# A decoder layer's FFN head reordered: the shift written to the result at the end, pair 3's first weights loaded two tiles later, pair 2's X and Y worked on behind h's last row tile

## The chip, the cores and the metric

The kernel runs on one core of a Trainium2 chip. The metric is the device time of one execution in microseconds (us). The core has these engines: TensorE (PE in the profile; PEld is its weight load), VectorE (DVE), ScalarE (ACT), GpSimd (POOL) and SyncE (SP). SP, ACT and POOL also issue DMA transfers; each of them has a queue of its own that is worked off in order, and all queues share 16 DMA engines. A name with a q behind it (SPq, POOLq) is an engine's instruction queue.

## What is computed

One layer of a decoder on an input of 512 tokens by 1024 channels, float32:

```
proj = x @ w_in                       # q, k, v, pool_in, gate logits
y_attn = moba_attention(q, k, v) @ w_branch_attn
y_pool = multiscale_pool(pool_in) @ w_branch_pool
mixed = sigmoid(g0) * y_attn + sigmoid(g1) * y_pool
h = layer_norm(ALPHA * x + mixed @ w_out, ln1_g, ln1_b)
a, u = split(h @ w_ffn_in)            # 2 x 2816 columns
a = causal_dwconv(a, conv_w, conv_b)  # width 3
f = (gelu(a) * u) @ w_ffn_out
out = layer_norm(ALPHA * h + f, ln2_g, ln2_b)
```

The last line adds the row `ln2_b` to every row of the result. In this text that row, repeated over all tokens, is called the shift.

## The kernel before

**Precision.** Every float32 operand is split into a high part (`hi`, rounded by ScalarE at L76) and a low part (`lo`, the difference, taken by VectorE at L77). A product is then three matmuls, high by high, high by low and low by high (`mm3`, L246; L248, L251 and L252 in the profile).

**Weights.** All weights of the layer are cut into tiles of 128 x 1024 (512 KB) and numbered in the order of use in the list `chunks`. `fetch` (L135) takes the next one: it issues the load into a raw tile on SP (L151), and splits it into a slot of a ring of five pairs (`RING`). Raw tiles have the tag `wraw`, with three slots; raw tiles of the plain weights (`wraw` in the profile) and of the A weights of pairs (`araw`) share them. `weights(i)` fetches up to three tiles ahead of tile i (`LEAD`), but not past `state["limit"]`.

**Pairs.** Most weight tiles come in pairs whose two products are made with seven half-size products in place of eight (a Strassen scheme, `seven`, L293). A pair (key `("f", n)` in the FFN) needs four tiles from its two raw halves: A, X, D and Y. A is a plain load into an `araw` tile (`fetch_raw`, L188). X is a difference, made by two loads into one tile: a plain one on SP (L196), and an adding one on POOL (L198). D is half a tile, loaded on SP (L190). Y needs no load; it is made from X and A by two VectorE additions (L212). A's raw tile is kept until Y has been made in it. `load_ahead(i)` (L158) issues the raw loads of pairs ahead of tile i: A up to 4 tiles, X up to 5, D up to 6 (`AHEAD`), except for keys with a number of their own in `EARLY`. For A the number counts only where the pair before also is a pair, else it is 0. The other operand's forms, called T1 to T4, are made on VectorE and split (`t_form`, L266).

**The FFN's head.** After the attention and the merge, the product with `w_out` is made in four row tiles of 128 tokens (`wo_mm`). Row tile i is normalised on VectorE (`ln1_vec`, L833), then transposed on TensorE into `hT`, split, and copied to `hraw` (`ln1_T`, L843). During the last row tile's product the first five FFN tiles are fetched: pair 2's A, and then four plain tiles (0 to 3, columns a and u of FFN blocks 0 and 1). Four plain tiles are multiplied in two halves of the tokens: first with t1 (row tiles 0 and 1; L934 to L938), later with t2 (row tiles 2 and 3; L954 to L957). Between the halves stand pair 2's A (`seven_open`) and row tile 3's transposition (L940). `h_forms(r)` makes the four forms of one half of h's rows: `h_forms(0)` uses row tiles 0 and 2, `h_forms(1)` row tiles 1 and 3. Then all pairs from 2 to 18 follow (L965).

**What sets the order.** The program is handed to a scheduler which orders each engine's instructions by their place in the program and by when its own model of time has them ready. Two means write an order by hand: `tc.issue_after(ins)`, in which every instruction made on `ins`'s engine stands behind `ins` in that engine's queue, and `tc.keep_in_program_order`. Loads can be placed far ahead of their place in the program; that holds for the write of the shift at L931, which has nothing to wait for.

**The FFN's end.** `w_ffn_out` is multiplied in seven products (`product`, L1038), with weights partly loaded on SP (L231, `wraw<-in_w_fo`) and partly made in the tile `tw` by adding loads on POOL (L236). `ln_rows(2)` (L758) loads the scale and shift rows of the second norm, repeated over 128 partitions, into the tile `lnb` on POOL, and POOL scales the first of them (L761). The result's row tiles 0 and 1 are finished early: `scale_out` (L807) scales the centred rows on ScalarE and adds them to the result in memory with an adding DMA on POOL (L812), which is why the shift must stand in the result's first 256 rows before. Row tiles 2 and 3 add the shift on the core (L820, L829, L803) and are stored by SP and ACT (L1065).

Of the kernel before, what the change touches and what calls it, by code (L numbers as in the profile page):

```python
# [14 lines left out]
P = 128  # L15
S = 512
D = 1024
# [14 lines left out]
LEAD = 3  # L32
RING = 5
# [10 lines left out]
HALVED = 2 * SEVEN[0]  # L44
TAILED = 2
AHEAD = {"A": 4, "X": 5, "D": 6}
EARLY = {("i", 1, "X"): 3, ("i", 1, "D"): 2, ("i", 2, "A"): 3, ("i", 2, "X"): 2, ("i", 2, "D"): 3}
SUMMED = (("i", 1),)
PRODUCTS = ("T3", "B11", "B21", "T1", "T2", "B22", "T4")

# [2 lines left out]
def layer_kernel(ctx: ExitStack, tc: tile.TileContext, xT, x, w_v, w_c, rel_bias, invcnt, w_group,  # L53
                 pscale, w_br, w_out, lnr, w_fi, convp, w_fo, out):
    nc = tc.nc
# [9 lines left out]
    def bank(name):  # L65
        return ps.tile([P, S], F32, tag="ps", name=name)
# [5 lines left out]
    def split(hi, lo, src, copy=None):  # L72
        if copy:
            copy(hi, src)
        else:
            state["hi"] = nc.scalar.activation(hi, src, AF.Copy)  # L76
        state["lo"] = nc.vector.tensor_tensor(lo, src, hi.bitcast(F32), op=ALU.subtract)  # L77
        return state["lo"]
# [5 lines left out]
    at = {}  # L84
    pair_of = {}
# [25 lines left out]
    FI0 = len(chunks)  # L111
# [16 lines left out]
    def slot(i, n, near=False):  # L128
        o = BESIDE if near else 0
        return tuple(wp.tile([P, SLOT], F32R, tag=f"w{q}", name=f"w{q}{i}", bufs=RING)[:, o:o + n]  # L130
                     for q in ("hi", "lo"))

    state = {"next": 0, "limit": WO0 - 1}

    def fetch(pool=None, early=None):  # L135
        i = state["next"]
        state["next"] = i + 1
        load_ahead(i)
        if isinstance(chunks[i], tuple):
            ready[i] = (fetch_fo if i >= FO0 else fetch_seven)(i, *chunks[i])  # L140
            return
        raw = wp.tile([P, D], F32, tag="wraw", name=f"wraw{i}", bufs=3)
        if pool is None:
            hi, lo = slot(i, D, FI0 < i <= FI0 + HALVED)
        else:
            hi = pool.tile([P, D], F32R, name=f"whi{i}")
            lo = pool.tile([P, D], F32R, name=f"wlo{i}")
        parts = 2 if early else 1
        for c in range(parts):
            sl = slice(c * (D // parts), (c + 1) * (D // parts))  # L150
            (nc.scalar if early else nc.sync).dma_start(raw[:, sl], chunks[i][:, sl])  # L151
            split(hi[:, sl], lo[:, sl], raw[:, sl])
            if c == 0 and early:
                state["w0"] = raw[:, sl]
                early()
        ready[i] = (hi, lo)

    def load_ahead(i):  # L158
        for q, ahead in AHEAD.items():
            while coming[q]:  # L160
                key = coming[q][0]
                n, f = key
                lead_ = EARLY.get((n, f, q), ahead)
                if not homes.get((n, q)) or at[n, f, q] > i + (lead_ if q != "A" or (n, f - 1) in pair_of else 0):
                    break
                with ExitStack() as held:
                    if (n, f, q) == ("i", 1, "X"):
                        held.enter_context(tc.issue_after(state["neg"].ins))
                    if (n, f, q) in (("i", 1, "D"), ("i", 2, "A"), ("i", 2, "X"), ("i", 2, "D")):
                        held.enter_context(tc.issue_after(state["plain"].ins))  # L170
                    if (n, f, q) == ("i", 2, "X"):
                        held.enter_context(tc.issue_after(state["sum"].ins))
                    fetch_raw(coming[q].pop(0), q)
# [8 lines left out]
    homes = {(n, "A"): araw for n in "igf"}  # L182

    def fetch_raw(key, q):
        a, u = pair_of[key]
        r = raws[key, q] = homes[key[0], q](key[1])
        if q == "A":
            nc.sync.dma_start(r, a)  # L188
        elif q == "D":
            nc.sync.dma_start(r, u[:, S:])  # L190
        elif key in SUMMED:
            state["plain"] = nc.sync.dma_start(r[:, :S], u[:, :S])
        else:
            v = r.rearrange("p (a c) -> p a c", a=2)
            (pst, pn), (est, _) = u.ap
            state["plain"] = nc.sync.dma_start(  # L196
                v, bass.AP(tensor=u.tensor, offset=u.offset, ap=[[pst, pn], [0, 2], [est, S]]))
            state["acc"] = nc.gpsimd.dma_start(  # L198
                v, bass.AP(tensor=a.tensor, offset=a.offset, ap=[[pst, pn], [u.offset + S - a.offset, 2], [est, S]]),
                accum_op=ALU.add)  # L200
# [40 lines left out]
    def weights(i):  # L241
        while state["next"] <= min(i + LEAD, state["limit"]):
            fetch()
        return ready[i]
# [41 lines left out]
    def seven_open(key, whole, y):  # L286
        ba, bc = (bank(f"s{q}{key[0]}{key[1]}") for q in "ac")
        s_mm(key, "A", 0, block(whole, k1, t1), ba[:, 256:], True)
        nc.scalar.activation(y, ba[:, 256:], AF.Copy)
        s_mm(key, "A", 1, block(whole, k2, t1), bc[:, :256], True)  # L290
        return ba, bc
# [314 lines left out]
    ap = attn.enter_context(tc.tile_pool(name="ap", bufs=2, reuse_waits="tile"))  # L606
# [109 lines left out]
    def gate_done(f, ba, u):  # L716
        if f < KT - 1:
            for br, v, scale in ((0, ba, 1.0), (1, u, -1.0)):
                nc.scalar.activation(v, v, AF.Sigmoid, scale=scale)
                nc.vector.tensor_tensor(branch[f, br], branch[f, br], v, op=ALU.mult)  # L720
            merged(f, branch[f, 0], branch[f, 1])
        else:
            for br, v, scale in ((0, ba, 1.0), (1, u, -1.0)):
                gslot[8 * br + f] = unused.pop(0)
                nc.scalar.activation(gslot[8 * br + f], v, AF.Sigmoid, scale=scale)
# [6 lines left out]
    for f in range(GSEVEN, KT):  # L732
        if f == KT - 1:
# [3 lines left out]
              lambda ba, u, f=f: gate_done(f, ba, u), first_half if f == KT - 1 else None)  # L737
# [20 lines left out]
    def ln_rows(r):  # L758
        t = hw.tile([P, 2, D], F32, tag="lnb", name=f"lnb{r}")
        nc.gpsimd.dma_start(t, bass.AP(tensor=lnr.tensor, offset=lnr.offset + r * D, ap=[[0, P], [D, 2], [1, D]]))  # L760
        nc.gpsimd.tensor_scalar(t[:, 0, :], t[:, 0, :], -0.5, None, op0=ALU.mult)  # L761
        return t

    lnb = ln_rows(0)
# [78 lines left out]
    def ln1_T(i):  # L843
        for n in range(2):
            b = bank(f"ht{i}_{n}")
            for k in range(4):
                kt = 4 * n + k
                nc.tensor.transpose(b[:, k * P:(k + 1) * P], xs[:, i, kt * P:(kt + 1) * P], ident)
            b = b.rearrange("p (a c) -> p a c", a=4)
            split(hT_hi[:, 4 * n:4 * n + 4, i * P:(i + 1) * P], hT_lo[:, 4 * n:4 * n + 4, i * P:(i + 1) * P], b)  # L850
            nc.scalar.activation(hraw[:, 4 * n:4 * n + 4, i * P:(i + 1) * P], b, AF.Copy)
# [30 lines left out]
    def fi_mm(j, b, t):  # L882
        wh, wl = split3(weights(at["f", j // 2, "au"[j % 2]]), KT)
        for kt in range(KT):
            mm3(b[:, t], (wh[:, kt, :], wl[:, kt, :]), (hT_hi[:, kt, t], hT_lo[:, kt, t]), kt == 0, kt == KT - 1)
# [41 lines left out]
    coming["X"], late_x = [k for k in coming["X"] if k[1] in firsts], [k for k in coming["X"] if k[1] not in firsts]  # L927
    coming["D"], late_d = [k for k in coming["D"] if k[1] in firsts], [k for k in coming["D"] if k[1] not in firsts]
    load_ahead(FI0 + HALVED)
    shift = bass.AP(tensor=lnr.tensor, offset=lnr.offset + 3 * D, ap=[[0, 2 * P], [1, D]])  # L930
    nc.gpsimd.dma_start(out[:2 * P, :], shift)  # L931
    hb = {}
    head_f = SEVEN[0]
    for j in range(HALVED):  # L934
# [3 lines left out]
            ln1_T(2)  # L938
    opened = seven_open(("f", head_f), (hT_hi, hT_lo), homes["f", "P"](head_f))
    ln1_T(3)  # L940

    rows = [slice(r * P, r * P + P) for r in range(2)]

    def h_forms(r):
        blocks_ = [hraw[:, k, t.start + rows[r].start:t.start + rows[r].stop] for k in (k1, k2) for t in (t1, t2)]
        for n in parts:
            t_form(n, {n: tuple(v[:, :, rows[r]] for v in tt[n])}, *blocks_)

    with tc.issue_after(state["norm"].ins):
        h_forms(0)  # L950
        state["limit"] = FI0 + RING
        fetch()
    h_forms(1)
    for j in range(HALVED):  # L954
        state["limit"] = FI0 + RING + 1 + j
        weights(state["limit"] - LEAD)
        fi_mm(j, hb[j], t2)  # L957
        if j % 2:
            gated(j // 2, hb[j - 1], hb[j])
# [98 lines left out]
    def gather_all(bs, *parts):  # L1058
        for i in range(2):
            for row, col, sign, first, last in parts:  # L1060
                gather(2 * row + i, col * S, (col + 1) * S, bs[i], sign, first, last)
# [19 lines left out]
    gather(3, S, D, bank_a[1], 1, False, False)  # L1081
    product(5, bank_d, False)
    lnb = ln_rows(2)
    gather_all(bank_d, (0, 0, -1, False, True))
    for i in range(2):
        scale_out(i)
# [86 lines left out]
```

## Time and profile before

| | |
|---|---|
| time, median of 3 executions (lowest, highest) | 636.46 us (634.88, 636.7) |
| the profiled execution's own time | 635.43 us |
| its span, from the first instruction to the last | 633.6 us |
| instructions | 10413 |
| mean granted clock of TensorE in it | 0.992 |
| moved by DMA | 107.70 MB, mean 170 GB/s |

Times in the profile count from the start of the span. A row of the timeline holds the start, the duration, the engine, the line of the code, the operation, the tile written, the tiles read, the number of instructions of one kind that are merged in it, and in brackets the engine's idle time ahead of it and what ended that. A row of the list of waits holds the engine and the line that waited, what it waited for, the sum of the waits, their number, and the longest. A row of the windows holds the stretch and its length, the busy time of each engine in it with the number of instructions, the clock granted to TensorE as a share of the full one, the mean busy share of the DMA engines, and what they moved in GB/s. A row of the DMA issues holds what was loaded into what, the queue, the number, the size and the median time from issue to landing. The granted clock of the page is given for 40 equal slices of the span, in tenths; 9 stands for 90% and more.

### The profile page before, as it was taken

The numbers are of one execution on the slowest core, as the hardware profiler recorded it, in microseconds if no ns is written. First come the engines' busy times: TensorE is split into PE (matmuls) and PEld (weight loads), VectorE is DVE, ScalarE is ACT, GpSimd is POOL, SyncE is SP. The second block draws the span as 40 slices with busy tenths as digits, with TensorE's granted clock in tenths as the row PEclk, the third lists the DMA queues.
The fourth block names the chain that finished last, engine by engine and source line by source line (L and its number), as shares of the span: only waits on it lengthen the run. The fifth ranks groups of instructions, "written<-read, shape, count | busy, mean of one in ns | idle before, by whom it ended". The sixth has DMA issues, their size and how long they took to land.

```text
span 633.6 us, 10413 instructions
## 1 busy us (share of the span) xinstructions
PE 619.3 (98%) x3988; PEld 554.9 (88%) x3988; DVE 506.9 (80%) x780; ACT 354.4 (56%) x536; POOL 120.7 (19%) x132
## 2 busy tenths in 40 slices
PE   7999999999999999999899999999999999999994
PEld 4889998777788998889899999999999888888884
DVE  4988887786395788399798888899888869798886
ACT  4746677656544567124476656666656456555542
POOL 1033123433133111110011011011000302123302
PEclk9999999999999999999899999999999999999997
DMA  8667738422438615805548686777744996889805
GB/s 302 216 190 177 200 104 230 134 69 99 149 103 219 163 55 180 302 31 180 120 136 209 173 193 189 190 190 204 184 115 136 326 268 127 201 200 207 198 1 132
DMA packets 40529, 107.70 MB, mean 170 GB/s; under 512 B 4368, under 2 KB 4632, under 8 KB 40224
## 3 DMA queue, kind: packets, MB, share of 16 engines
q1 hardware_dynamic: 26976, 70.85, 33.7%
q0 software_dynamic: 12928, 35.15, 28.1%
q10 hardware_dynamic: 576, 1.05, 0.5%
q8 instruction: 31, 0.51, 0.3%
q14 instruction: 18, 0.15, 0.1%
HBM read 102.82 MB, written 3.17 MB: 167 GB/s over the span
## 4 chain that ended last, share of the span: by engine, by line
PE 94%; DMA 3%; DVE 2%; ACT 1%; SPq 0%; issue 0%; DVEq 0%; ACTq 0%
PE saf L248 5%; PE saf L252 5%; PE saf L251 5%; PE sbf L248 3%; PE sbf L251 2%; PE sbf L252 2%; PE fi L251 2%; PE br L248 2%; PE g L248 2%; PE g L252 2%; PE fi L252 2%; PE g L251 2%; PE fi L248 2%; PE br L251 2%; PE br L252 2%; PE wo L252 2%
## 5 line engine op out<-in xcount | busy, mean ns | idle before, releaser
L76 ACT ACTIVATE whi<-wraw 128x1024 fp32r<-128x1024 f32 (+1 forms) x53 | 53.8, 1022 | 44.5 <-DMA wraw<-in_w_fo 8.0
L77 DVE TENSOR_TENSOR wlo<-wraw,whi 128x1024 fp32r<-128x1024 f32 (+1 forms) x53 | 65.5, 1244 | 14.0 <-ACT whi L76 13.8
L77 DVE TENSOR_TENSOR wlo<-araw,whi 128x1024 fp32r<-128x1024 f32 x52 | 63.5, 1228 | 8.7 <-ACT whi L76 8.2
L76 ACT ACTIVATE whi<-araw 128x1024 fp32r<-128x1024 f32 x52 | 54.6, 1058 | 18.6 <-PE saf L251 5.5
L198 POOL DMA_DIRECT2D xraw<-in_w_fi x15 | 18.1, 1203 | 141.7 <-DVE fT L307 37.0
L76 ACT ACTIVATE whi<-tw 128x1024 fp32r<-128x1024 f32 (+1 forms) x30 | 29.5, 983 | 24.9 <-DMA tw<-in_w_fo 9.9
L77 DVE TENSOR_TENSOR wlo<-tw,whi 128x1024 fp32r<-128x1024 f32 (+1 forms) x30 | 33.5, 1129 | 8.2 <-ACT whi L76 8.1
L248 PE MATMUL fi<-hT_hi,whi 128*128 128x256 f32 (+1 forms) x112 | 36.2, 328 | 2.1 <-ACT whi L76 2.1
L251 PE MATMUL saf<-hT_lo,whi 128*128 128x256 f32 x136 | 38.0, 279 | 0.0
L248 PE MATMUL saf<-hT_hi,whi 128*128 128x256 f32 x136 | 38.0, 279 | 0.0
L248 PE MATMUL sbf<-T_hi,whi 128*128 128x256 f32 x136 | 37.9, 279 | 0.0
L252 PE MATMUL saf<-hT_hi,wlo 128*128 128x256 f32 x136 | 37.9, 279 | 0.0
L248 PE MATMUL saf<-nT_hi,whi 128*128 128x256 f32 x136 | 37.8, 278 | 0.0
L252 PE MATMUL saf<-nT_hi,wlo 128*128 128x256 f32 x136 | 37.8, 278 | 0.0
L251 PE MATMUL sbf<-T_lo,whi 128*128 128x256 f32 x136 | 37.7, 277 | 0.0
L251 PE MATMUL saf<-nT_lo,whi 128*128 128x256 f32 x136 | 37.7, 277 | 0.0
L252 PE MATMUL sbf<-T_hi,wlo 128*128 128x256 f32 x136 | 37.7, 277 | 0.0
L251 PE MATMUL fi<-hT_lo,whi 128*128 128x256 f32 (+1 forms) x112 | 36.4, 327 | 0.2 <-DVE hT_lo L77 0.2
L252 PE MATMUL fi<-hT_hi,wlo 128*128 128x256 f32 (+1 forms) x112 | 36.4, 326 | 0.0
L563 POOL TENSOR_SCALAR pp<-pp,rs 128x128 f32<-128x128 f32 (+3 forms) x32 | 25.8, 820 | 36.1 <-DVE rs L560 28.3
L236 POOL DMA_DIRECT2D tw<-in_w_fo x18 | 15.6, 895 | 62.1 <-DVE wlo L77 61.9
L558 ACT ACTIVATE pp<-pp,nm 128x128 f32<-128x128 f32 (+3 forms) x32 | 17.6, 552 | 14.8 <-DVE nm L555 14.8
(347 smaller groups left out, 2178.9 us busy)
## 6 DMA issues: line engine op xcount, KB each, us to landing
tw<-in_w_fo POOLq DMA_DIRECT2D x20, 512.0 KB, 7.8
araw<-in_w_fi SPq DMA_DIRECT2D x17, 512.0 KB, 3.3
xraw<-in_w_fi SPq DMA_DIRECT2D x15, 512.0 KB, 4.0
xraw<-in_w_fi POOLq DMA_DIRECT2D x15, 512.0 KB, 6.0
wraw<-in_w_c SPq DMA_DIRECT2D x10, 512.0 KB, 4.8
wraw<-in_w_fi SPq DMA_DIRECT2D x10, 512.0 KB, 3.6
wraw<-in_w_fo SPq DMA_DIRECT2D x10, 512.0 KB, 4.7
tw<-in_w_fo SPq DMA_DIRECT2D x10, 512.0 KB, 7.1
```

The source lines that it names most:

```text
L76: state["hi"] = nc.scalar.activation(hi, src, AF.Copy)
L77: state["lo"] = nc.vector.tensor_tensor(lo, src, hi.bitcast(F32), op=ALU.subtract)
L198: state["acc"] = nc.gpsimd.dma_start(v, bass.AP(tensor=a.tensor, offset=a.offset, ap=[[pst, pn], [u.offset + S - a.offset, 2], [est, S]]), ...
L236: nc.gpsimd.dma_start(raw, half(then[1:], sl), accum_op=ALU.add)
L248: ins = nc.tensor.matmul(out_, wh, ah, start=start, stop=False, **kw)
L251: nc.tensor.matmul(out_, wh, al, start=False, stop=False, **kw)
L252: nc.tensor.matmul(out_, wl, ah, start=False, stop=stop, **kw)
L558: exps[h] = nc.scalar.activation(pp[:, offs[i]:offs[i] + n], pp[:, offs[i]:offs[i] + n], AF.Exp, bias=nm[:, i:i + 1], accum_out=rs[:, i:i ...
L563: nc.gpsimd.tensor_scalar(pp[:, offs[i]:offs[i] + n], pp[:, offs[i]:offs[i] + n], rs[:, i:i + 1], 1.0, op0=ALU.mult, op1=ALU.mult)
```

## The change

It has three parts.

1. The shift is no longer written to the result's first 256 rows by one DMA from memory to memory on POOL (L931). Behind the sixth product, once `lnb` has been loaded, two DMAs on SP write it from `lnb[:, 1, :]`, 128 rows each.
2. `EARLY` gets an entry for pair 3's A, 2. `load_ahead` counts an entry of `EARLY` in full, also for A; for all other keys the number stays what it was. So pair 3's A, which was loaded while the fifth FFN tile was fetched, is loaded while the seventh is fetched.
3. The first fetch of pair 2's X ahead of the t2 half, which stood between `h_forms(0)` and `h_forms(1)`, is taken out; the loop over the four plain tiles fetches X with D. All fetches of that loop (X, D and Y of pair 2, A and X of pair 3) are put behind the two last split instructions of `ln1_T(3)` on ScalarE and on VectorE (`turned`).

```diff
 AHEAD = {"A": 4, "X": 5, "D": 6}
-EARLY = {("i", 1, "X"): 3, ("i", 1, "D"): 2, ("i", 2, "A"): 3, ("i", 2, "X"): 2, ("i", 2, "D"): 3}
+EARLY = {("i", 1, "X"): 3, ("i", 1, "D"): 2, ("i", 2, "A"): 3, ("i", 2, "X"): 2, ("i", 2, "D"): 3,
+         ("f", 3, "A"): 2}
...
             while coming[q]:
                 key = coming[q][0]
                 n, f = key
-                lead_ = EARLY.get((n, f, q), ahead)
-                if not homes.get((n, q)) or at[n, f, q] > i + (lead_ if q != "A" or (n, f - 1) in pair_of else 0):
+                lead_ = EARLY.get((n, f, q), ahead if q != "A" or (n, f - 1) in pair_of else 0)
+                if not homes.get((n, q)) or at[n, f, q] > i + lead_:
                     break
...
     load_ahead(FI0 + HALVED)
-    shift = bass.AP(tensor=lnr.tensor, offset=lnr.offset + 3 * D, ap=[[0, 2 * P], [1, D]])
-    nc.gpsimd.dma_start(out[:2 * P, :], shift)
     hb = {}
...
     ln1_T(3)
+    turned = state["hi"].ins, state["lo"].ins
...
     with tc.issue_after(state["norm"].ins):
         h_forms(0)
-        state["limit"] = FI0 + RING
-        fetch()
     h_forms(1)
     for j in range(HALVED):
         state["limit"] = FI0 + RING + 1 + j
-        weights(state["limit"] - LEAD)
+        with tc.issue_after(turned[0]), tc.issue_after(turned[1]):
+            weights(state["limit"] - LEAD)
         fi_mm(j, hb[j], t2)
...
     product(5, bank_d, False)
     lnb = ln_rows(2)
+    for i in range(2):
+        nc.sync.dma_start(out[i * P:(i + 1) * P, :], lnb[:, 1, :])
     gather_all(bank_d, (0, 0, -1, False, True))
     for i in range(2):
         scale_out(i)
```

## The prediction, made before the changed kernel was run

> **What bounds the kernel now.** First the engine table, the clock row and the chain on the page, then the list of TensorE's waits.
>
> ```profile
> PE 619.3 (98%) x3988; PEld 554.9 (88%) x3988; DVE 506.9 (80%) x780; ACT 354.4 (56%) x536; POOL 120.7 (19%) x132
> ...
> PEclk9999999999999999999899999999999999999997
> ...
> PE 94%; DMA 3%; DVE 2%; ACT 1%; SPq 0%; issue 0%; DVEq 0%; ACTq 0%
> ```
> ```profile
> PE fi L248 <- ACT whi L76: 2.1, 1, 2.1
> PE v L425 <- ACT whi L76: 2.0, 1, 2.0
> ```
>
> TensorE (PE) works 98% of the span and 94% of the chain that ended last is its work. So only its gaps can be won: a wait for split weights in the first product (2.0 us), one in the FFN's head (2.1), and slice 20, where the clock reads 8 tenths. Whatever PE gains early it keeps, unless a supplier falls behind.
>
> **Part 1a: the shift leaves the start.** Written at L931, it was issued at the very start. The rows are from the timeline, the DMA issues, the chain and the windows (last two columns: DMA share, GB/s).
>
> ```profile
> 1.43 0.82 POOL L931 DMA_DIRECT2D out<-in_lnr  x1 [0.36 <-issue]
> ...
> out<-in_lnr POOLq DMA_DIRECT2D x1, 1024.0 KB, 9.8
> ...
> 2.66 9.18 DMA wraw<-in_w_v
> 11.86 1.06 ACT whi L76
> ...
> 6.00:8.00 2.00, 2.00 (x10) 1.62 (x9) 1.37 (x3) 0.63 (x1) 0.00 (x0) 1.00 1.04 336
> ...
> 9.02 1.07 PE L425 MATMUL v<-whi,xT_lo 128*128 128x512 f32 x4
> 9.93 1.07 PE L425 MATMUL v<-wlo,xT_hi 128*128 128x512 f32 x4
> 12.97 1.21 PE L425 MATMUL v<-whi,xT_hi 128*128 128x512 f32 x4 [1.97 <-ACT whi L76]
> ```
>
> The shift is in flight from 1.4 to about 11.2 us, when the DMA engines are full (share 1.04). Its 1.05 MB at 336 GB/s is 3.1 us of transfer. The weight load that PE waits for lands at 11.84; without the shift at about 8.7, and its split ends by 9.8. PE's last four matmuls before that wait start at 9.93; the four before took 0.91 (from 9.02), so PE would go on at 10.84, instead of at 12.97. That is **2.1 us**. The input tiles land some 3 us earlier too, so VectorE's forms, which follow them, move at least as far as PE. Ends: 0, if the load waits for something else than bytes, and 3.1, if the matmuls before it hurry as well; I take 2.1, the gap itself.
>
> **Part 2: pair 3's A loads later.** In the FFN's head: SP's queue with the landing times of its two L151 loads (one is before these rows), VectorE's split of plain tile 2, and PE.
>
> ```profile
> 291.02 0.33 SPq L188 DMA_DIRECT2D araw<-in_w_fi  x1
> 293.77 0.89 SPq L196 DMA_DIRECT2D fT<-in_w_fi  x2
> 294.70 1.62 SPq L190 DMA_DIRECT2D fT<-in_w_fi  x2
> 296.42 0.65 SPq L151 DMA_DIRECT2D wraw<-in_w_fi  x1
> ...
> DMA to landing us min/median/max: 3.3/5.4/7.5
> ```
> ```profile
> 294.71 1.21 DVE L77 TENSOR_TENSOR wlo<-wraw,whi 128x1024 fp32r<-128x1024 f32 x1
> ```
> ```profile
> 302.67 0.28 PE L252 MATMUL fi<-hT_hi,wlo 128*128 128x256 f32 x1
> 305.08 0.39 PE L248 MATMUL fi<-hT_hi,whi 128*128 128x256 f32 x1 [2.13 <-ACT whi L76]
> ...
> 306.55 0.42 PE L248 MATMUL saf<-hT_hi,whi 128*128 128x256 f32 x1
> 309.55 0.39 PE L252 MATMUL scf<-hT_hi,wlo 128*128 128x256 f32 x1
> ...
> 313.20 0.62 PE L248 MATMUL fi<-hT_hi,whi 128*128 128x256 f32 x4
> 314.01 0.39 PE L251 MATMUL fi<-hT_lo,whi 128*128 128x256 f32 x1 [0.19 <-DVE hT_lo L77]
> ```
>
> Raw tiles have three slots, and pair 2's A keeps one. The slot that comes free at 291.0 goes to pair 3's A. Plain tile 3 (the last L151) has to wait for the next, free at 294.71 + 1.21 = 295.92; it goes out at 296.42 behind two X and two D loads and takes the 7.5 us of the landing row, to 303.9. That is PE's wait. After the change tile 3 takes the slot at 291.0, on an idle queue, like the L151 load with 3.3 us: it lands at about 294.4 and is split by 297 (if VectorE does it last in the head, PE waits some 0.6 us more). Pair 3's A goes out where tile 3 did: no byte is added, SP has no other load behind it that is due, and its tile is used only after pair 2.
>
> Behind the wait the clock is halved. From 314.01 to pair 2's X at 324.75 (row below) PE starts 92 matmuls, one in 0.117 us; from 306.55 to 309.55 it starts 14, one in 0.214. That costs 3.00 - 14 x 0.117 = 1.4 us. [...]
>
> **Part 3: X and Y behind h's last row tile.** What is late next is row tile 3: its transposes now directly precede the t2 matmuls, with no plain tile 3 left between them. Its latency is that of row tile 2:
>
> ```profile
> 296.36 1.04 PE L848 MATMUL ht<-ident,xs 128*128 128x128 f32 x8
> ...
> 297.62 0.69 DVE L77 TENSOR_TENSOR hT_lo<-ht,hT_hi 128x512 fp32r<-128x512 f32 x1 [0.41 <-ACT hT_hi L76]
> ...
> 297.15 0.36 PE L248 MATMUL fi<-hT_hi,whi 128*128 128x256 f32 x1
> ```
>
> The first half's low part is ready 1.95 us after the first transpose (297.62 + 0.69 - 296.36). After the change: PE ends tile 2 at 302.79, tile 3 takes 24 x 0.117 = 2.81, pair 2's A as much, so the transposes start at 308.4. They take 0.8 (296.36 to 297.15), four hT_hi matmuls 0.5, and the first hT_lo matmul comes at 308.4 + 1.95 = 310.4, after a pause of 0.7 us. Before it came at 314.01. The gain of parts 2 and 3 is **3.6 us**: the wait, the halved clock and the old pause, less the new pause. It needs VectorE to split row tile 3 at once. That is what part 3 sees to: X's split and Y's sums, in these rows, now stand behind it.
>
> ```profile
> 306.33 0.69 DVE L212 TENSOR_TENSOR araw<-fT,araw 128x512 f32<-128x512 f32 x1
> ...
> 310.92 1.23 DVE L77 TENSOR_TENSOR wlo<-fT,whi 128x1024 fp32r<-128x1024 f32 x1 [1.50 <-ACT whi L76]
> ...
> 304.00:308.00 4.00, 2.92 (x18) 2.92 (x19) 2.90 (x4) 1.94 (x3) 0.00 (x0) 0.80 1.05 201
> 312.00:316.00 4.00, 3.81 (x33) 3.61 (x33) 4.00 (x8) 2.70 (x5) 0.00 (x0) 1.00 0.01 4
> ...
> 324.75 0.28 PE L248 MATMUL sbf<-T_hi,whi 128*128 128x256 f32 x1
> ```
>
> PE reaches pair 2's X 10.74 us after the first hT_lo matmul, by these rows, so at 321.1, and Y 12 matmuls later, at 322.5. Behind the wait VectorE has: hT_lo 2 x 0.69, X 1.23, Y's sums 2 x 0.69, eight form and split steps of row tile 3 of about 0.69, D 0.69, Y 1.23, in all 11.4 us from 309.7, so until 321.1, in the order of need: covered by 1.4 us. The cost I take is 0; the upper end is in the slower rival.
>
> **Part 1b: the shift at the end.** Two SP writes of 512 KB from lnb.
>
> ```profile
> 587.34 3.71 POOL L761 TENSOR_SCALAR lnb<-lnb 128x1024 f32<-128x1024 f32 x1 [5.30 <-DMA lnb<-in_lnr]
> ...
> 593.89 0.33 SPq L231 DMA_DIRECT2D wraw<-in_w_fo  x1
> ...
> 592.00:596.00 4.00, 4.00 (x19) 3.31 (x18) 3.83 (x6) 2.92 (x4) 0.81 (x1) 1.00 1.01 265
> ...
> 600.73 0.64 ACT L76 ACTIVATE whi<-wraw 128x512 fp32r<-128x512 f32 x1 [4.44 <-DMA wraw<-in_w_fo]
> ...
> 609.22 0.69 DVE L1053 TENSOR_TENSOR xs<-xs,fod 128x512 f32<-128x512 f32 x1 [1.31 <-PE fod L252]
> ...
> 619.37 0.88 POOL L812 DMA_DIRECT2D out<-xs  x1 [26.56 <-ACT xs L811]
> ```
>
> lnb lands at 587.3, with the DMA engines full until about 600; the writes cost 1.05 MB / 265 GB/s = 4.0 us of transfer. At worst they stand before the last weight load: it lands at 604.7 instead of 600.7, its split (some 1.6 us) ends at 606.3, and PE needs it for the last six matmuls of the product that ends at about 609, so at 607.6. The adding stores (L812), queued on POOL ahead of the last rows' additions, now wait for the writes, which land by 605, 14 us before 619.4. Cost 0, with 1.3 us to spare; bounds 0 and 2.7, if the load is late by the whole 4.0 more.
>
> **Sum.** 2.1 + 3.6 = 5.7 us. The profiled execution took 635.43 (span 633.6 and 1.8 around it): 629.7. The median of the three runs, 636.46, lies 1.0 higher: 630.8. Forecast: between them, **630.2**. The rivals' times start from the middle too, 636.0.
>
> **Rivals.**
> - **Start only** (the FFN wait returns, as the pause at row tile 3 or at pair 2's X, again with a halved clock). For: VectorE is full from 312 on. Against: 1.4 us of cover at Y. Time: 636.0 - 2.1 = 633.9.
> - **FFN only** (the first loads are held by latency or by their slots). For: SP's loads queue one behind another. Against: share 1.04. Time: 636.0 - 3.6 = 632.4.
> - **The clock's loss is in few runs.** For: nearly the same idle time did not halve it at the start. Against: the profiled execution, which has the loss, is not slower than the median. Then 1.4 us less is won: 630.2 + 1.4 = 631.6.
> - **Nothing**: both gaps come back elsewhere, or the loads keep their order: 636.
> - **Slower**: VectorE becomes the bound behind row tile 3. If the 11.4 us of work and the two gates (each three steps of some 0.7, so 4.2) run at the rate of 304 to 308, 2.90 busy of 4.00, they take 15.6 / 0.725 = 21.5, to 331.2, and Y, due at 322.5, stops PE for 8.7 us; with the clock's 1.4 that is 10.1 lost against 5.7 won: 640.4. It decides from a stop of about 4.3 us. Against: from 312 to 316 VectorE works without a gap.
>
> **How the numbers follow.** Forecast 0.55, clock 0.12, start only 0.12, FFN only 0.09, nothing 0.06, slower 0.06. The range goes from 628.4 (the start's upper end, and some of the new pause hidden) to 634.4 (start only, against the median); outside lie nothing, slower, and some 0.06 of tails. About 0.3%, 1.9 us, is what a measurement tells from no change; start only lies on that edge, half of it counts as the same: faster 0.82, same 0.12, slower 0.06.
>
> **What would show it.** In the changed profile: no L931 near 1.4 us, the wait at v L425 gone, and matmuls running on at about 10.8; SP's last L151 at about 291 and pair 3's A behind the X and D loads; no wait at fi L248 and no 0.8 in the clock row; a pause under 1 us at row tile 3; at the end, out<-lnb on SP, landed before 606. Wrong would be a PE wait over 1 us at sbf or saf between 318 and 326, the clock at half again, or a start as before.

## The result, and the profile after

| | before | changed |
|---|---|---|
| time, median (lowest to highest), first comparison | 636.58 us (634.88 to 638.31), 4 runs | 628.73 us (628.32 to 629.35), 4 runs |
| ratio, 95% interval | | 0.9877 (0.9849 to 0.9906) |
| profiled execution, its span | 635.43, 633.6 | 629.03, 627.3 |
| all comparisons with the experiments | 635.64 us (632.43 to 640.25), 58 runs | 629.25 us (628.32 to 630.51), 16 runs |

The change makes the kernel faster by 7.9 us in the first comparison, and by 6.4 us if all runs are taken together (the 58 runs are those beside the experiments, the 16 those of the first comparison and of the two experiments that run the changed kernel unaltered). 630.2 was forecast, with 628.4 to 634.4 as the range.

Line numbers from L48 on to about L930 are one higher in the changed kernel: v L425 is L426, fi L248 is L249, the SP load L151 is L152. The engine table, the clock row and the chain of its page:

```profile
PE 617.3 (98%) x3988; PEld 553.3 (88%) x3988; DVE 505.0 (81%) x780; ACT 354.0 (56%) x536; POOL 118.5 (19%) x131
...
PEclk9999999999999999999999999999999999999998
...
PE 98%; DVE 1%; DMA 1%; ACT 0%; DVEq 0%; issue 0%
```

Its list of TensorE's waits, whole (warm_ps is the start of the program, the same 1.2 us before and after):

```profile
PE warm_ps L341 <- DVE warm L338: 1.2, 1, 1.2
PE fi L249 <- ACT hT_hi L77: 0.2, 1, 0.2
```

Both waits of two microseconds are gone, and so is the 8 in the clock row. TensorE is now 98% of the chain instead of 94%. Its timeline at the places of the old waits, and at pair 2's X:

```profile
9.87 1.07 PE L426 MATMUL v<-wlo,xT_hi 128*128 128x512 f32 x4
10.78 1.07 PE L426 MATMUL v<-whi,xT_hi 128*128 128x512 f32 x4
...
305.82 1.03 PE L849 MATMUL ht<-ident,xs 128*128 128x128 f32 x8
307.11 0.74 PE L249 MATMUL fi<-hT_hi,whi 128*128 128x256 f32 x4 [0.25 <-ACT hT_hi L77]
318.61 0.28 PE L249 MATMUL sbf<-T_hi,whi 128*128 128x256 f32 x1
```

The product v runs on at 10.78, where it stopped until 12.97 before. Pair 2's X begins at 318.61 instead of 324.75: 6.1 us earlier, which stays to the end. What makes it possible stands on SP's queue, first in the FFN's head, then in the last products:

```profile
288.26 1.52 SPq L152 DMA_DIRECT2D wraw<-in_w_fi  x2
291.24 0.89 SPq L197 DMA_DIRECT2D fT<-in_w_fi  x2
292.18 0.94 SPq L191 DMA_DIRECT2D fT<-in_w_fi  x2
294.03 23.70 SPq L189 DMA_DIRECT2D araw<-in_w_fi  x3
...
581.56 0.87 SPq L1084 DMA_DIRECT2D out<-lnb  x2
582.52 5.52 SPq L232 DMA_DIRECT2D wraw<-in_w_fo  x3
```

Plain tiles 2 and 3 (L152) go out back to back, and pair 3's A (among the araw loads that are merged in the row of 294.03) behind X and D. At the end the two stores of the shift stand ahead of the last three weight loads.

Where the time of each kernel goes can be read from five starts in TensorE's timeline: the first matmul of product p, the first fi and the first foe (the FFN's pairs lie between), the first fod, and the last matmul of all. Between the first p and the first fi nothing is touched, except that e6 and e11 have the copy there. The table has the profiles of all kernels, those of the experiments too:

| kernel | copy at the start | first p | first fi to first foe | first fod to last matmul |
|---|---|---|---|---|
| before | yes | 29.46 | 226.15 | 60.20 |
| changed | no | 27.09 | 222.49 | 60.21 |
| e1, part 1 alone | no | 27.09 | 223.91 | 60.21 |
| e2, part 2 alone | yes | 29.65 | 229.50 | 60.21 |
| e3, part 3 alone | yes | 31.54 | 226.22 | 60.20 |
| e4, parts 2 and 3 | yes | 31.33 | 222.49 | 60.21 |
| e5, copy doubled | doubled | 34.98 | 226.73 | 60.21 |
| e6, copy in the middle | no | 26.51 | 222.49 | 60.20 |
| e7, row tile 3 earlier | no | 27.20 | 221.87 | 60.21 |
| e8, changed again | no | 26.59 | 222.49 | 61.27 |
| e9, e10, changed with an addition | no | 27.40, 26.57 | 222.49, 222.46 | 60.35, 60.21 |
| e11, e6 and e7 together | no | 27.12 | 222.38 | 60.21 |
| e12, changed again | no | 26.94 | 222.47 | 60.82 |

### The profile page after: what moved, and what is told of

Same layout as the page of the kernel before. It is cut to its first block, busy times and chain, and to the rows that moved or that the text cites. A ratio compares the mean times of both kernels' runs of the same rounds, so it can differ in the third digit from the quotient of the medians.

```text
span 627.3 us, 10417 instructions
## 1 busy us (share of the span) xinstructions
PE 617.3 (98%) x3988; PEld 553.3 (88%) x3988; DVE 505.0 (81%) x780; ACT 354.0 (56%) x536; POOL 118.5 (19%) x131
## 3 DMA queue, kind: packets, MB, share of 16 engines
q10 hardware_dynamic: 576, 1.05, 0.5%
## 4 chain that ended last, share of the span: by engine, by line
PE 98%; DVE 1%; DMA 1%; ACT 0%; DVEq 0%; issue 0%
PE saf L252 5%; PE saf L249 5%; PE saf L253 5%; PE fi L249 3%; PE fi L252 3%; PE v L426 3%; PE fi L253 3%; PE sbf L252 3%; PE sbf L253 2%; PE sbf L249 2%; PE br L249 2%; PE g L249 2%; PE g L253 2%; PE g L252 2%; PE br L252 2%; PE wo L252 2%
## 5 line engine op out<-in xcount | busy, mean ns | idle before, releaser
L249 PE MATMUL saf<-nT_hi,whi 128*128 128x256 f32 x136 | 37.8, 278 | 0.0
L249 PE MATMUL saf<-hT_hi,whi 128*128 128x256 f32 x136 | 37.8, 278 | 0.0
L249 PE MATMUL sbf<-T_hi,whi 128*128 128x256 f32 x136 | 37.7, 277 | 0.0
L249 PE MATMUL fi<-hT_hi,whi 128*128 128x256 f32 (+1 forms) x112 | 36.2, 328 | 0.2 <-ACT hT_hi L77 0.2
```

What stands on the lines that cost most here:

```text
L249: ins = nc.tensor.matmul(out_, wh, ah, start=start, stop=False, **kw)
```

## The experiments

The theory: the start's copy and the FFN's late plain tile are two separate losses, with the clock's half behind the second; part 3 gains nothing by itself, but keeps row tile 3 from becoming the next wait. The first rivals: one part does it all, or part 3 isn't needed. The first four kernels ran on one chip, with 29 runs of the kernel before at 635.68 us (633.08 to 640.12).

**e1: part 1 alone.**

```diff
-    shift = bass.AP(tensor=lnr.tensor, offset=lnr.offset + 3 * D, ap=[[0, 2 * P], [1, D]])
-    nc.gpsimd.dma_start(out[:2 * P, :], shift)
...
     lnb = ln_rows(2)
+    for i in range(2):
+        nc.sync.dma_start(out[i * P:(i + 1) * P, :], lnb[:, 1, :])
```

> The kernel before with part 1 alone (shift written at the end from lnb). Theory (two separate gaps): the start's gap goes, PE passes from the third weight tile on 2.2 to 2.5 us earlier, the FFN's wait stays at about 2 us: 2.5 us faster than before. Rival (the shift's bytes only move the wait): under 1 us faster. Rival on the clock (its halving behind the FFN's wait is chance): the profile shows the wait of some 2 us at fi with no stretch of PE clock at half behind it; the theory expects some 3.4 us at half again.

Measured: 630.53 us (629.92 to 632.3, 6 runs), ratio 0.9912 (0.9882 to 0.9941), so 5.2 us faster, twice what was expected. The list of TensorE's waits in its profile still has the FFN's, but shorter:

```profile
PE fi L248 <- ACT whi L76: 1.4, 1, 1.4
```

In this profile the clock is not halved behind it, and all six runs have a mean clock of .996 or .997. By the table the start gave 2.4 us against the profile of before; the FFN's head, which part 1 doesn't touch, was 2.2 us shorter as well (223.91 against 226.15). So one profile doesn't size this wait: it is longer or shorter, and halves the clock or doesn't. Whether that is chance is open. The three profiles with the copy at the start and plain tile 3 late (before, e3, e5) have 2.1 to 2.8 us there, all with the clock halved; e1, without the copy, is the only one with less. Part 1 may therefore shorten the FFN's wait too, which no run here tells apart from a draw.

**e2: part 2 alone.** The diff is the entry in `EARLY` and the two lines of `load_ahead`.

> The kernel before with part 2 alone (pair 3's A loaded two tiles later). Theory: plain tile 3 is issued at about 291 and the FFN's wait of 2.1 us and the halved clock go; without part 3, pair 2's X may be split ahead of h's row tile 3, so the pause at row tile 3 is 0.7 to 2 us: 2.3 to 3.6 us faster than before. Rival (part 2 does nothing without part 3): a pause over 3 us at row tile 3, and no gain.

Measured: 639.42 us (637.51 to 641.75, 12 runs), ratio 1.0057 (1.0034 to 1.008): slower, against the expectation, and with the sign that its rival named, a pause of over 3 us at row tile 3. The wait on plain tile 3 is gone, and a longer one has come; the timeline at the start's wait and around the new one, and the windows (the column before the last two is the clock):

```profile
13.19 1.19 PE L426 MATMUL v<-whi,xT_hi 128*128 128x512 f32 x4 [2.84 <-ACT whi L77]
...
308.35 1.03 PE L849 MATMUL ht<-ident,xs 128*128 128x128 f32 x8
...
308.94 0.69 DVE L213 TENSOR_TENSOR araw<-fT,araw 128x512 f32<-128x512 f32 x1 [4.91 <-DMA fT<-in_w_fi]
...
312.62 1.04 ACT L77 ACTIVATE whi<-fT 128x1024 fp32r<-128x1024 f32 x1
...
314.08 1.06 ACT L77 ACTIVATE hT_hi<-ht 128x512 fp32r<-128x512 f32 x2
...
314.71 1.22 PE L249 MATMUL fi<-hT_hi,whi 128*128 128x256 f32 x4 [5.32 <-ACT hT_hi L77]
```
```profile
14.00:16.00 2.00, 2.00 (x10) 1.67 (x9) 1.80 (x4) 1.48 (x3) 0.00 (x0) 1.00 0.95 339
...
312.00:316.00 4.00, 1.22 (x4) 0.93 (x4) 4.00 (x7) 3.07 (x5) 0.00 (x0) 0.50 0.00 0
316.00:320.00 4.00, 3.76 (x22) 3.76 (x23) 3.83 (x7) 2.88 (x5) 0.00 (x0) 0.65 0.01 4
```

TensorE has transposed row tile 3 by 309.4. But on VectorE the sum for pair 2's Y stands first and waits 4.91 us for X to land; the forms behind it, ScalarE's splits of them and of X (312.62) and only then hT_hi (314.08) follow. The clock is halved in and behind these 5.32 us (but not behind the 2.84 at the start), and the FFN's stretch is 7.0 us longer than the changed kernel's.

**e3: part 3 alone.** The early fetch of X is taken out, and the fetches of the t2 loop stand behind `turned`.

> The kernel before with part 3 alone (X, D, Y of pair 2 behind row tile 3's split). Theory: the wait for plain tile 3 stays at 2.1 us, the small pause at hT_lo goes: 0 to 0.4 us faster, the same within the measurement. Rival (part 3 carries the gain of the head): 2 us or more faster. Clock: the theory expects the stretch at half again behind the wait; if chance, it may be missing.

Measured: 636.66 us (632.16 to 638.27, 12 runs), ratio 0.9984 (0.9956 to 1.0011): no difference. The wait on plain tile 3 is untouched; its timeline and its windows:

```profile
13.49 1.66 PE L425 MATMUL v<-whi,xT_hi 128*128 128x512 f32 x4 [1.85 <-ACT whi L76]
...
307.86 0.58 PE L248 MATMUL fi<-hT_hi,whi 128*128 128x256 f32 x1 [2.81 <-ACT whi L76]
```
```profile
14.00:16.00 2.00, 2.00 (x6) 1.53 (x6) 1.90 (x3) 1.32 (x2) 0.00 (x0) 0.50 0.99 368
16.00:18.00 2.00, 2.00 (x8) 1.56 (x7) 1.74 (x2) 1.87 (x4) 0.00 (x0) 0.64 0.99 327
```

Here the clock is halved behind the start's wait too, although that wait was no longer than in the profile of before.

**e4: parts 2 and 3, the copy left at the start.**

> Parts 2 and 3 without part 1 (the shift still at 1.4 us). Theory: 3.6 us faster than before, the start's wait of 2.0 us as before; with e1 the two sum to the whole change. Rival (the parts need each other): e1 and e4 sum to less than 5 us or more than 9.

Measured: 633.49 us (632.07 to 635.43, 12 runs), ratio 0.9962 (0.9941 to 0.9984), 2.2 us faster where 3.6 was expected. The FFN's stretch is that of the changed kernel, 222.49. The start's wait and the clock behind it, from the timeline and the windows:

```profile
13.25 1.21 PE L426 MATMUL v<-whi,xT_hi 128*128 128x512 f32 x4 [3.01 <-ACT whi L77]
```
```profile
14.00:16.00 2.00, 2.00 (x7) 1.57 (x7) 1.78 (x4) 1.46 (x3) 0.00 (x0) 0.68 0.99 325
16.00:18.00 2.00, 2.00 (x6) 1.53 (x5) 2.00 (x3) 1.98 (x4) 0.00 (x0) 0.50 0.93 337
18.00:20.00 2.00, 2.00 (x10) 1.62 (x9) 2.00 (x3) 1.99 (x3) 0.00 (x0) 0.97 0.97 286
```

So each loss can be removed without the other: e1 gives 5.2, e4 gives 2.2, in all 7.3, and the whole change 6.4 to 7.9. That they simply add up is not shown as closely as it looks: e1's interval alone goes from 3.8 to 7.5 us. Part 2 alone costs 3.7 us, with part 3 it gains 2.2: part 3 is worth 5.9 us, but only behind part 2.

The next four kernels ran on one chip with 17 runs of the kernel before at 635.83 us.

**e5: the copy doubled**, a test of what the start's wait is made of.

```diff
     nc.gpsimd.dma_start(out[:2 * P, :], shift)
+    nc.gpsimd.dma_start(out[2 * P:, :], shift)
```

> The kernel before, with the start's copy doubled: the second half of the result is also written at the start by the same GpSimd queue, 2 MB in place of 1 MB (these rows are written again at the end, as before). If the wait at the first v product is the copy's bytes taking the load engines' time from w_v, that wait grows from 1.9-3.0 us (four profiles with the copy) to between 3 and 6 us, and the time from about 636 to 637-640 us. If only the copy's being there counts (its place on the queue, one descriptor), wait and time stay: 1.9-3.0 us and 634-638 us. A longer wait may also bring the halved clock behind it in every run rather than in some; then the runs lie at 638 us and above with hardly any spread.

Measured: 640.08 us (637.09 to 646.22, 12 runs), ratio 1.0056 (1.0025 to 1.0088). Its timeline, and the windows behind the wait:

```profile
15.68 2.07 PE L425 MATMUL v<-whi,xT_hi 128*128 128x512 f32 x4 [5.31 <-ACT whi L76]
```
```profile
14.00:16.00 2.00, 0.32 (x1) 0.32 (x2) 0.34 (x1) 1.06 (x1) 0.00 (x0) 0.75 0.95 308
16.00:18.00 2.00, 2.00 (x6) 1.52 (x6) 1.32 (x2) 1.05 (x2) 0.00 (x0) 0.50 1.02 407
18.00:20.00 2.00, 2.00 (x6) 1.61 (x5) 0.96 (x3) 1.32 (x3) 0.00 (x0) 0.50 0.95 323
20.00:22.00 2.00, 2.00 (x6) 1.52 (x6) 2.00 (x3) 1.98 (x4) 0.00 (x0) 0.54 0.83 306
```

Another 1 MB lengthens the wait by 3.3 us against the profile of before (5.31 and 1.97), and by 2.3 against the longest of the others (3.01). The prediction's 3.1 us of transfer for 1.05 MB lies between: the wait grows with the copy's bytes, and does not come from the copy's being there alone. The expectation that the halving then comes in every run was wrong: the twelve runs have mean clocks from .989 to .997, and the run at .997 (639.59 us) leaves no room for a halved stretch, which takes .0027 off.

**e6: the shift in neither place**, copied from memory to memory behind POOL's scaling of the first norm's rows, where the changed kernel moves nothing (DMA share 0.00 from 272 to 280).

```diff
-        nc.gpsimd.tensor_scalar(t[:, 0, :], t[:, 0, :], -0.5, None, op0=ALU.mult)
+        state["scaled"] = nc.gpsimd.tensor_scalar(t[:, 0, :], t[:, 0, :], -0.5, None, op0=ALU.mult)
...
+    with tc.issue_after(state["scaled"].ins):
+        shift = bass.AP(tensor=lnr.tensor, offset=lnr.offset + 3 * D, ap=[[0, 2 * P], [1, D]])
+        nc.gpsimd.dma_start(out[:2 * P, :], shift)
...
-    for i in range(2):
-        nc.sync.dma_start(out[i * P:(i + 1) * P, :], lnb[:, 1, :])
```

> The changed kernel, but the 1 MB for the first half of the result is copied in the middle (GpSimd's queue, behind its scaling of the first norm's rows, near 273 us of the span) in place of being stored from SBUF near the end. The theory that the end's two stores are free (margin of 1.3 us by the trace of before) says 628.3-629.4 us, as the changed kernel. The rival that they cost something in the last loads says up to 2.7 us less, 626-628 us. If the copy hurts wherever weights are loaded, the products near 273-295 us wait and the time is 630-632 us.

Measured: 628.98 us (628.47 to 629.89, 6 runs). It goes out at 272.84; its row of the DMA issues:

```profile
out<-in_lnr POOLq DMA_DIRECT2D x1, 1024.0 KB, 6.7
```

It lands in 6.7 us instead of the 9.8 that it took at the start, and TensorE waits for nothing there: from the first p to the first fi it takes 263.96 us, as in the changed kernel. In time it can't be told from e8, the changed kernel beside it (629.24, 628.79 to 630.26, 6 runs).

**e7: row tile 3 ahead of pair 2's A.**

```diff
-    opened = seven_open(("f", head_f), (hT_hi, hT_lo), homes["f", "P"](head_f))
     ln1_T(3)
     turned = state["hi"].ins, state["lo"].ins
+    opened = seven_open(("f", head_f), (hT_hi, hT_lo), homes["f", "P"](head_f))
```

> The changed kernel with row tile 3 of h transposed and split before the first half of pair 2's A products is issued, not after it. The remaining wait there (0.25 us on ScalarE's split in the trace of the changed kernel, with the halved pace of nothing behind it) goes: 0.2-0.5 us faster, 628.2-628.5 us. The rival: the norm of row tile 3 isn't done that early, TensorE waits in front of the transposes for VectorE, some 1-4 us, and the time is 630-633 us.

Measured: 628.85 us (627.48 to 629.41, 6 runs). The timeline of TensorE:

```profile
303.12 1.03 PE L849 MATMUL ht<-ident,xs 128*128 128x128 f32 x8
303.91 0.36 PE L249 MATMUL saf<-hT_hi,whi 128*128 128x256 f32 x1
...
306.77 0.63 PE L249 MATMUL fi<-hT_hi,whi 128*128 128x256 f32 x4
```

Pair 2's A follows the transposes, and t2 follows without a wait. The FFN's stretch is 0.62 us shorter, a little more than the 0.2 to 0.5 expected. In the times, 0.4 us between medians with ranges that overlap, it isn't shown.

**e8: the changed kernel again**, beside these three.

> The changed kernel unaltered, on the same chip as the three others, to compare them with: 628.3-629.4 us in every run if the spread of the kernel before (633-640 us) came from its two waits, which are gone; a spread of 3 us or more if it comes from elsewhere.

Measured: 629.24 us, with a spread of 1.5 us, where the kernel before spread over 7.7 on that chip; two of the six runs lie above the 629.4 that was expected at most. But its profile has a wait that the first profile of the changed kernel hasn't, at the end (timeline, then the DMA issues of 575 to 610):

```profile
596.33 1.62 ACT L77 ACTIVATE whi<-wraw 128x1024 fp32r<-128x1024 f32 x2 [1.07 <-DMA wraw<-in_w_fo]
...
600.29 0.50 PE L252 MATMUL fod<-wlo,sd_hi 128*128 128x512 f32 x1 [0.77 <-DVE wlo L78]
```
```profile
out<-lnb SPq DMA_DIRECT2D x2, 512.0 KB, 6.6
...
wraw<-in_w_fo SPq DMA_DIRECT2D x2, 512.0 KB, 9.6
...
wraw<-in_w_fo SPq DMA_DIRECT2D x1, 256.0 KB, 10.0
```

The last weight loads of the product take 9.6 and 10.0 us from issue to landing, and TensorE waits for VectorE's split of the second to last one. In the first profile of the changed kernel these loads took 8.0 and 7.9, and nothing waited.

**e9 and e10: a stall of TensorE by itself**, to see whether idle time alone halves the clock; K is 1 in e9 and 2 in e10, `state["v1"]` the last matmul of the k tile before, and the added matmul adds zeros.

```diff
...
+            if kt == 2:
+                with tc.issue_after(state["v1"].ins):
+                    for _ in range(K):
+                        nc.gpsimd.memset(pause, 0.0)
+                tc.keep_in_program_order(nc.tensor.matmul(bs[0][:, :64], pause[:, :P], pause[:, P:P + 64],
+                                                          start=False, stop=False))
...
```

> The changed kernel with a stall of TensorE put in by itself: ahead of the third k tile of v a 128x64 matmul of zeros waits for a GpSimd memset (128x1024) that starts only when the second k tile is done; nothing else is moved, no bytes are added. Estimated wait about 1.0-1.5 us. If a wait costs its length alone, every run is 1.0-1.5 us above the changed kernel of the same chip (about 630.5), with a spread of 1-2 us. If the halved clock also follows waits this short, some runs lie 1.5-2 us higher still, at a granted clock .002-.003 lower.

> The same with two memsets one behind the other, an estimated wait of 2.0-2.7 us, as long as the waits that the copy at the start made (1.9-3.0 us in four profiles). If the halved clock is a matter of chance behind such a wait, whatever causes it, the runs fall in two groups: about 631.3 us at a clock of .995-.997, and about 633 us at .993-.994; the spread is 2.5 us or more. If the halving came from the copy or from the loads and not from the idle, all runs lie at about 631.3 us.

Measured: 628.96 us (628.18 to 630.02, 6 runs) and 629.53 us (628.78 to 630.01, 5 runs), beside e12 at 629.55. The stall did not come about. The timeline of POOL in e10:

```profile
0.96 0.95 POOL L424 MEMSET pause<- 128x1024 bf16 x1
...
2.25 0.94 POOL L424 MEMSET pause<- 128x1024 bf16 x1
```

`issue_after` orders only the engine of the instruction that it is given, which is TensorE; the memsets on POOL were done by 3.2 us. So both are the changed kernel with one small matmul more, and the question isn't answered by them. The trace of e2 answers a part of it: there the clock is at half from 312 on (0.99 from 308 to 312, 0.50 from 312 to 316), in the middle of a wait (309.4 to 314.7) in which the DMA engines fall idle (share 0.36 from 308 to 312, and 0.00 from 312 to 316). So in this one case neither the copy, issued at the start, nor busy DMA engines stood beside the halved clock.

**e11: e6 and e7 together**, and **e12: the changed kernel** beside it.

> The changed kernel with both alterations of e6 and e7: the first half of the result copied in the middle on GpSimd's queue, and row tile 3 of h transposed and split ahead of pair 2's A. If the 0.55-0.75 us by which TensorE is earlier in the profile of e7, and the wait of 0.8 us before the last down products in the profile of e8 (absent in e6), are real, it is 0.5-1.2 us faster than the changed kernel beside it (628.0-628.6 against 629.2). If they are the spread of single profiles, the two agree within 0.3 us.

> The changed kernel unaltered, on the same chip as the three others: 628.3-630.3 us with a spread of 2 us or less. It is the base from which the stalls of e9 and e10 and the gain of e11 are taken.

Measured: e11 628.13 us (628.07 to 629.72, 4 runs), e12 629.55 us (628.65 to 630.51, 6 runs). Three of e11's four runs lie below all six of e12, the fourth among them; its profile is of that fourth run, and shows no wait of TensorE but the first. It is the best of the versions by its median, 1.4 us below e12; that it is better than the changed kernel is likely, and not settled by four runs. Against before it is 0.9892 (0.9874 to 0.991).

## Why the prediction was right, point by point

**Start (part 1a, 2.1 us): right in mechanism; its size left out the clock.** The first p comes at 26.5 to 27.4 in the nine profiles without the copy, 26.95 in the mean, and at 29.46 and 29.65 in two with it whose clock stays full: 2.5 to 2.7 us. With the clock halved behind the wait it is 31.33 and 31.54, so 4.4 to 4.6 us. The prediction had no term for a halved clock at the start, since the clock row of its one profile read 9 there. By whole runs the start is worth 5.2 us (e1 against before) or 4.2 (the changed kernel, 629.25, against e4).

**FFN head (parts 2 and 3, 3.6 us): right for the profile.** There the stretch shrank by 3.66 us, from 226.15 to 222.49. The steps came as stated: plain tile 3 out at the slot's release, A behind X and D, no halved clock, a pause at row tile 3. That pause is 0.25 us where 0.7 was predicted. The terms that the prediction lists for its 3.6 (2.13, 1.4 and 0.19, less 0.7) add up to only 3.0; the 3.6 itself came from the two starts of the first hT_lo matmul, 314.01 and 310.4. The clock's 1.4 is a little too small, since it counts 3.0 us of a halved stretch of 3.4, which at the two paces measured there (0.214 and 0.117 us a matmul) costs 1.55. By whole runs the head is worth less, 2.2 us (e4) or 1.3 (the changed kernel against e1): the wait was 1.38 in e1, 2.13 in before and 2.81 in e3 and e5, and it doesn't halve the clock each time. So the two terms were off in opposite directions, the start's too small by 2 us or more and the head's too large by 1.4 us or more, and their sum, 5.7, stands against 6.4. That the forecast came so close is in part luck; in the first comparison, with 628.73, it was 1.5 us off and 0.3 inside the range.

**Part 3 as the cover.** The prediction put row tile 3 next in line and part 3 as what keeps X and Y from standing ahead of it. e2 shows the price without it: 5.32 us of wait, and a kernel slower than before. With it VectorE did not become the bound; the slower rival fell, and so did the rival that the FFN's wait comes back, at row tile 3 or at pair 2's X.

**Shift at the end (part 1b, 0 with bounds of 0 and 2.7): right at its bounds, and not always 0.** The stores stand ahead of the last three loads, not only of the last, and the two of them with 512 KB land after 8.0 to 10.4 us, where they took 4.8 before. The stretch from the first fod to the last matmul is 60.20 or 60.21 in all seven profiles without the stores. In the seven with them it is 60.21 in four, and 60.35, 60.82 and 61.27 in e9, e12 and e8. Mean cost 0.26 us, up to 1.1. So the margin of 1.3 us can be used up, as the prediction's upper bound allowed for; the most that it cost is less than half of that bound.

**The rival of the clock** (the loss behind the FFN's wait is in few runs) **is left open; another loss, which the prediction put at nothing, counted for more.** The mean clock of the 58 runs of the kernel before shows that most of them lose something:

| mean granted clock | runs | median (lowest to highest), us |
|---|---|---|
| .996, .997 | 13 | 633.89 (632.43 to 635.66) |
| .992 to .995 | 30 | 635.53 (633.64 to 638.62) |
| .987 to .991 | 15 | 638.93 (637.12 to 640.25) |

A line through the 58 runs falls by 0.67 us for each .001 of clock; 633.6 us of span times .001 is 0.63. So most of the spread of 7.8 us is the clock's (within a group 3 to 5 us are left). The profiled executions give the scale: without a halved stretch the mean clock was .997 (changed) and .996 (e1), with one of 3.4 us .992 (before) and .993 (e4), with two .992 (e3), with one of 6.9 us .991 (e2), and with 6.8 and 3.4 us .989 (e5); the mean takes in the end of the span too, where the clock reads 0.50 behind the last matmul in the profiles of before and changed. A halved stretch of 3.4 us takes .0027 off the mean clock of a span of 633.6 us, so that by this estimate the three runs at .987 had more than two of them. Below .995 lie 42 of the 58 runs, and 8 of the 12 of e4, which has only the start's wait; of e1, which has only the FFN's, and that shorter, none of six. By this the start's wait accounts for most of the loss. In how many runs the FFN's wait halves the clock stays open: it does in all three profiles that have both waits. The rival's time, 631.6, was missed because the start gained more than forecast. The changed kernel has neither wait, its 16 runs have a clock of .995 to .998, and its spread is 2.2 us. Of the 6.4 us some 4.6 are the waits themselves (from 633.89, the median of the runs at .996 and .997, to 629.25), and the other 1.75 the clock's.

## What to carry to other kernels

A copy that has nothing to wait for can be scheduled first, as this one was (issued at 1.43 us), and share the DMA engines with the loads that the first product needs (share 1.04 from 6 to 8 us; TensorE waited 1.85 to 3.01 us in the four profiles with it, 5.31 with its bytes doubled, and at that product not at all in that of the changed kernel): put it where the DMA is quiet, and look what is loaded behind it there. Take a load forward only with the queues of what it feeds in view: here the earlier tile alone made the kernel slower (e2, by 3.7 us), since another load, for which VectorE waited 4.91 us, stood ahead of the next operand in VectorE's and ScalarE's order. Size a TensorE wait by several profiles and by the clock of all runs: the FFN's wait was 1.38, 2.13, 2.81 and 2.81 us in the four profiles that have it.

## What the runs showed of the hardware

**Behind seven of the ten TensorE waits of over 1.3 us the granted clock was at half, for 3.4 us or about twice that.** For the profile of before, the windows of the FFN's head give it:

```profile
304.00:308.00 4.00, 2.92 (x18) 2.92 (x19) 2.90 (x4) 1.94 (x3) 0.00 (x0) 0.80 1.05 201
308.00:312.00 4.00, 4.00 (x30) 4.00 (x29) 2.50 (x4) 2.17 (x4) 0.00 (x0) 0.78 0.25 96
```

A clock of 0.80 over 4 us is 1.6 us at half, and 0.78 is 1.76: 3.4 us together. In the same trace, by windows of 0.01 us, the clock is at half from 306.36 to 309.77. In e3's start the rows above give 2.0 + 1.44 = 3.4, in e4's 1.28 + 2.0 + 0.12 = 3.4, and behind e5's 5.31 us it is 1.0 + 2.0 + 2.0 + 1.84 = 6.8. TensorE started a matmul of the same form every 0.214 us in the halved stretch of before and every 0.117 us behind it, so that 3.4 us at half cost about 1.55 us there. All ten waits, by their length:

| wait | length, us | granted clock around and behind it | at half, us |
|---|---|---|---|
| e1, FFN | 1.38 | 1.00 (304 to 308); one matmul in 0.117 us from 301.98 on | 0 |
| e3, start | 1.85 | 0.50 (14 to 16), 0.64 (16 to 18) | 3.4 |
| before, start | 1.97 | 1.00 (12 to 20) | 0 |
| before, FFN | 2.13 | 0.80 (304 to 308), 0.78 (308 to 312) | 3.4 |
| e3, FFN | 2.81 | 0.94 (304 to 308), 0.63 (308 to 312) | 3.4 |
| e5, FFN | 2.81 | 0.99 (308 to 312), 0.58 (312 to 316) | 3.4 |
| e2, start | 2.84 | 1.00 (12 to 20) | 0 |
| e4, start | 3.01 | 0.68 (14 to 16), 0.50 (16 to 18), 0.97 (18 to 20) | 3.4 |
| e5, start | 5.31 | 0.75 (14 to 16), 0.50 (16 to 20), 0.54 (20 to 22) | 6.8 |
| e2, FFN | 5.32 | 0.99 (308 to 312), 0.50 (312 to 316), 0.65 (316 to 320) | 6.9 |

By its length a wait doesn't tell: 1.85 us was followed by half the clock, and 2.84 was not. What decides between them is not shown. The profile of e5 has 6.8 us at half behind 5.31, while the mean clock of another run of e5, .997, leaves no room for a halved stretch; there is no profile of that run. The two kernels that were to test the waits by themselves made no stall.

**The same 1 MB copy cost the start 2.5 us or more and the middle nothing that shows.** At the start it landed in 9.8 us, among the first loads (DMA share 1.04 from 6 to 8 in the profile of before); in the middle in 6.7, where the DMA share with it is 0.44 from 272 to 276 and 0.48 from 276 to 280 (e6), and 0.00 in the changed kernel.
